# Mixture-of-experts products in units of 32 tokens over four column groups, tokens 33 to 64 under a branch

## The chip, the cores and the metric

The kernel runs on one core of one Trainium2 chip. The metric is the device time of one execution in microseconds (us), lower is better; the figure given for the kernel before is the median of three runs.

## What is computed

One layer of a hybrid network is applied to two groups of 128 tokens (a prompt and a sample), 256 tokens of width 1024 in all, in float32. Modulated norm, one input projection, three token mixers, gates, an output projection; then a second norm and a mixture of experts, a residual and a final norm. The part that the change touches is the mixture:

```python
logits = (t @ router_w + router_b).astype(F32)
top_v, top_i = lax.top_k(logits, TOP_K)            # 4 of 32 experts
probs = jax.nn.softmax(top_v, axis=-1)
...
gu = t @ wgu + bgu                                  # 1024 -> 2048
gate = jnp.minimum(gate, SWIGLU_LIMIT)
up = jnp.clip(up, -SWIGLU_LIMIT, SWIGLU_LIMIT)
act = (up + 1.0) * (gate * jax.nn.sigmoid(SWIGLU_ALPHA * gate))
out = act @ wdn + bdn                               # 1024 -> 1024
acc + wt[:, None].astype(t.dtype) * out
```

256 tokens with 4 experts each are 1024 places, 32 to an expert on average. The weights of one expert are 8 MiB (gate and up) and 4 MiB (down). The router of the reference, on the inputs that the reference draws by default, gives these token counts, in the order in which the kernel takes the experts (i = 0 to 31): 8, 45, 23, 21, 4, 32, 45, 46, 16, 25, 20, 70, 33, 34, 15, 10, 58, 73, 46, 28, 20, 9, 21, 15, 104, 14, 48, 28, 34, 40, 16, 23. Of i = 1 to 31, 18 experts have at most 32 tokens, 10 have 33 to 64 and 3 have more than 64 (i = 11, 17, 24).

## The kernel before

The first 340 us of the span compute everything up to the router. Then the experts follow one another (loop over `EXPERTS`, L1632 on). Their weights come in slabs of 1 MiB ([128, 2048] float32), 8 `gu` and 4 `dn` slabs an expert, all issued from SP in this order. The slabs go through a ring (`Ring`, L169): the slots of SBUF given to it by `start` and the `ring.give` lines are 0 to 11, 15 and 20 to 22, 16 slots. `ring.done` (L198) hands a slot back, and the next slab's DMA is issued on SP into it; that DMA waits for the last product that read the slot. So SP runs 16 slabs, one and a third experts, ahead of the slots that TensorE gives back.

TensorE (PE) takes the weights as the moving operand and the tokens as the stationary one. `gather` builds the expert's tokens, transposed, from `Pq`, a one-hot of the token's rank among the expert's tokens, for 64 ranks (`one_hots`, L1405). `gate_up` (L1491) with n = 64 uses the array as two column groups of 64: each of the four 512-column quarters of a slab is one product of 64 tokens, two of them side by side. With n = 32 it uses four column groups of 32. The products run in two halves of KS = 4 slabs (L1639). After each half `beyond` (L1621) asks for a register value `nu` (L1630, the number of further units of 32 tokens beyond the first 64): with nu = 0 nothing is done, with nu = 1 the stage `more_in` runs for 32 more tokens, with nu of 2 or more for 64 more. Then come `swiglu` (L1465, DVE and ACT), the transposition of the hidden values (`tr` and `copy` into `AT`, L1662), `down2` (L1517, n = 64: 64 columns, the two halves of the contraction in the two column groups), `beyond` with `more_out`, and `halves` (L1615), which scales the sums into a high and a low part; `scatter` (L1472) adds them to the tokens' sums in PSUM banks 4 to 7 one expert later. The first expert (i = 0, NR = 1) has a form of its own, `first_in`, without branches in it; all its tokens beyond 64 are done at the end (`all_once_more`, L1572, at i = 31).

Each branch stands on all engines. On PE, DVE and ACT the path that skips a body is a jump that first waits for the engine's own work before it (`UNCONDITIONAL_BRANCH [waits PE_49]` below).

## Time and profile before

| | us |
|---|---|
| median of 3 runs | 1371.79 (1369.27 to 1374.49) |
| the profiled execution | 1371.8 |
| its span (first to last instruction) | 1370.0 |
| PE busy in the span | 1247.5 (91%) |
| DVE, ACT busy | 418.2 (31%), 241.6 (18%) |
| HBM read | 472.61 MB, 346 GB/s over the span |
| mean granted TensorE clock | 0.981 of full speed |

In the trace PE is matrix products and PEld the loading of their stationary operand; SPq is SP's queue, which issues the DMAs. A float32 product of 512 columns shows as two records, so `gate_up` with n = 64 leaves 8 records a slab, and so does n = 32. L273 is the helper that records every product, L262 every transposition, L256 every DMA; which product it is has to be read from the tiles and shapes (`128*64 128x512` is 64 tokens against 512 columns).

### The profile page before, as it was taken

The numbers are of one execution on the slowest core, as the hardware profiler recorded it, in microseconds if no ns is written. First come the engines' busy times: TensorE is split into PE (matmuls) and PEld (weight loads), VectorE is DVE, ScalarE is ACT, GpSimd is POOL, SyncE is SP. The second block draws the span as 40 slices with busy tenths as digits, with TensorE's granted clock in tenths as the row PEclk, the third lists the DMA queues.
The fourth block names the chain that finished last, engine by engine and source line by source line (L and its number), as shares of the span: only waits on it lengthen the run. The fifth ranks groups of instructions, "written<-read, shape, count | busy, mean of one in ns | idle before, by whom it ended". The sixth has DMA issues, their size and how long they took to land. (4 is left out here: it accounts for less than half of the span.)

```text
span 1370.0 us, 18609 instructions
## 1 busy us (share of the span) xinstructions
PE 1247.5 (91%) x7146; PEld 645.4 (47%) x7146; DVE 418.2 (31%) x858; ACT 241.6 (18%) x490; POOL 42.1 (3%) x69
## 2 busy tenths in 40 slices
PE   5999789999999999999999999999999989999994
PEld 3677678898433344433334434243433343433331
DVE  7768769655111121111121112021211120211113
ACT  4463132233211111111111111011111100111111
POOL 1000101201000000000000000000000000000001
PEclk9999989999999999999999999999999999999997
DMA  9956796865899999999999999989999995999991
GB/s 278 339 180 216 115 318 232 259 242 219 333 384 417 367 415 417 415 415 415 416 401 370 415 416 417 415 346 402 417 415 414 414 395 193 412 414 415 415 407 41
DMA packets 124829, 477.02 MB, mean 348 GB/s; under 512 B 11871, under 2 KB 49505, under 8 KB 90864
## 3 DMA queue, kind: packets, MB, share of 16 engines
q1 hardware_dynamic: 121744, 468.25, 87.9%
q0 software_dynamic: 2288, 5.76, 1.4%
q8 instruction: 118, 1.93, 0.6%
q10 hardware_dynamic: 624, 0.63, 0.1%
q14 instruction: 55, 0.45, 0.1%
HBM read 472.61 MB, written 1.61 MB: 346 GB/s over the span
## 5 line engine op out<-in xcount | busy, mean ns | idle before, releaser
L273 PE MATMUL pb<-sl,sl 128*64 128x512 f32 (+5 forms) x5024 | 959.2, 507 | 32.1 <-PEq L1623 14.5
L273 PEld LDWEIGHTS pb<-sl,sl 128*64 128x64 f32 (+2 forms) x5024 | 431.9, 147 | 515.8 <-issue 450.5
L304 ACT ACTIVATE sl<-sl 128x512 f32<-128x512 f32 (+5 forms) x131 | 72.6, 564 | 559.2 <-DVE sl L279 496.0
L279 DVE TENSOR_SCALAR sl<-pb 128x512 f32<-128x512 f32 (+1 forms) x35 | 23.6, 676 | 434.5 <-PE pb L273 434.5
L287 DVE SCALAR_TENSOR_TENSOR sl<-pb,wsl,sl 128x512 fp32r<-128x512 f32 x64 | 47.6, 750 | 311.1 <-ACT sl L304 309.8
L304 ACT ACTIVATE sl<-pb 128x512 f32<-128x512 f32 (+6 forms) x125 | 68.6, 586 | 215.4 <-PE pb L273 194.0
L262 PE MATMUL pb<-cst,sl 128*128 128x128 f32 (+2 forms) x354 | 53.8, 282 | 28.1 <-DMA sl<-ssm_b_re 8.4
L304 ACT ACTIVATE sl<-pb,wsl 128x512 fp32r<-128x512 f32 x64 | 43.6, 688 | 201.7 <-PE pb L273 198.8
L273 PE MATMUL pb<-hb,sl 128*128 128x128 f32 x512 | 69.7, 291 | 8.4 <-DVE hb L291 8.0
L273 PE MATMUL pb<-sl,PT 128*128 128x512 f32 x256 | 76.3, 420 | 0.5 <-PEq L1623 0.5
L291 DVE TENSOR_TENSOR sl<-sl,sl 128x512 fp32r<-128x512 f32 (+3 forms) x80 | 65.1, 833 | 32.9 <-ACT sl L304 30.9
L273 PEld LDWEIGHTS pb<-hb,sl 128*128 128x128 f32 x512 | 65.8, 203 | 18.9 <-ACT wsl L304 12.7
L262 PEld LDWEIGHTS pb<-cst,sl 128*128 128x128 f32 (+2 forms) x354 | 40.5, 149 | 47.0 <-issue 14.3
L287 DVE SCALAR_TENSOR_TENSOR hb<-sl,taps,hb 128x256 f32<-128x256 f32 x120 | 49.8, 477 | 0.3
L273 PEld LDWEIGHTS pb<-sl,PT 128*128 128x128 f32 x256 | 45.1, 196 | 7.8 <-ACT sl L304 1.3
L291 DVE TENSOR_TENSOR sl<-PWT,sl 128x1024 f32<-128x1024 f32 x32 | 37.8, 1219 | 6.8 <-PE pb L273 6.7
L273 PEld LDWEIGHTS pb<-comb,hb 128*128 128x128 f32 x128 | 19.2, 202 | 43.9 <-DVE sl L279 41.3
L273 PE MATMUL pb<-comb,hb 128*128 128x1 f32 x128 | 21.6, 237 | 17.7 <-PEq L1623 15.9
L273 PE MATMUL pb<-ha,selb 128*64 128x512 bf16 (+1 forms) x140 | 21.4, 390 | 17.1 <-PEq L1623 14.0
L291 POOL TENSOR_TENSOR sl<-sl,sl 128x512 f32<-128x512 f32 (+3 forms) x11 | 16.4, 1503 | 671.3 <-DVE sl L291 656.4
L291 DVE TENSOR_TENSOR sl<-sl 128x512 f32<-128x512 f32 (+4 forms) x79 | 35.3, 464 | 4.5 <-ACT wsl L304 0.5
L273 PE MATMUL pb<-sl,cs 128*32 128x256 f32 (+1 forms) x320 | 30.4, 439 | 0.7 <-PEq L1623 0.7
(170 smaller groups left out, 403.9 us busy)
## 6 DMA issues: line engine op xcount, KB each, us to landing
sl<-w_gate_up SPq DMA_DIRECT2D x256, 1024.0 KB, 13.9
sl<-w_down SPq DMA_DIRECT2D x128, 1024.0 KB, 16.5
sl<-w_mod SPq DMA_DIRECT2D x24, 1024.0 KB, 9.6
sl<-w_in SPq DMA_DIRECT2D x20, 1024.0 KB, 10.8
sl<-w_out SPq DMA_DIRECT2D x4, 1024.0 KB, 12.9
sl<-md POOLq DMA_DIRECT2D x6, 512.0 KB, 9.0
sl<-w_four SPq DMA_DIRECT2D x2, 1024.0 KB
sl<-Kd SPq DMA_DIRECT2D x16, 128.0 KB, 9.0
```

Source lines behind the costliest of these rows:

```text
L262: return sch.op("P", 0.107 * in_.shape[0] / 128, [out], [in_], lambda: te.transpose(out, in_, ident[:in_.shape[0], :in_.shape[0]]))
L273: lambda: te.matmul(out, lhsT, rhs, start=start, stop=stop, skip_group_check=True))
L279: return sch.op(e, c, [o], ap, lambda: ENG[e].tensor_scalar(o, a, s1, None, op0=op0))
L287: lambda: ENG[e].scalar_tensor_tensor(o, a, sc, b, op0=op0, op1=op1))
L291: return sch.op(e, c, [o], [a, b], lambda: ENG[e].tensor_tensor(o, a, b, op=op))
L304: [a] + [x for x in (bias, scale) if hasattr(x, "tensor")], lambda: s.activation(o, a, func, **kw))
```

## The change

For i = 1 to 31 an expert's gate and up products run with n = 32, in one PSUM bank, and tokens 33 to 64 run as a second unit of 32 under a branch of their own (`nu > 0`), with their bias, their own half of the SwiGLU (`glu32(1)`) and of the transposition (`hidden(1)`). `nu` now counts the units beyond the first 32, so that the stages beyond 64 tokens stand under nu > 1 and nu > 2 and do what they did. The down products have two forms: `down2` with 64 columns where there are tokens 33 to 64, `down32` otherwise, which puts the sums of four parts of the contraction into four groups of 32 rows. For that `Pq` gets a second row of ones for experts of at most 32 tokens (`second_row`, four DVE operations per pair of experts, from `rank2` and `far`). The register of the next expert is loaded right after the SwiGLU of the present one (`later = units(...)`). The code of the first expert stays.

```diff
         tt(rank[:, :, :], PB[2][:, 0:64].rearrange("p (g e) -> p g e", g=2), self_[:, :, :], OP.add)
+        far = sm.tile([128, 32], F32, name="far", tag="zi")
+        ts(far[:, :], PB[2][:, 64:96], 32.0, 1000.0, op0=OP.is_gt, op1=OP.mult)
...
+        def second_row(b):
+
+            for a, e in enumerate(EXPERTS[2 * b:2 * b + 2]):
+                if 2 * b + a >= NR:
+                    for g in range(2):
+                        stt(Pq[:, b % 2, a, g], cst[:, C_IOTA:C_IOTA + 128], rank2[:, g, e:e + 1], Pq[:, b % 2, a, g],
+                            op0=OP.is_equal, op1=OP.add)
...
-            ts(nuf[:, :], cntf[:, :], 64.0, None, op0=OP.is_gt)
-            for u in range(1, 6):
-                stt(nuf[:, :], cntf[:, :], 64.0 + 32 * u, nuf[:, :], op0=OP.is_gt, op1=OP.add)
+            ts(nuf[:, :], cntf[:, :], 32.0, None, op0=OP.is_gt)
+            for u in range(1, 7):
+                stt(nuf[:, :], cntf[:, :], 32.0 + 32 * u, nuf[:, :], op0=OP.is_gt, op1=OP.add)
             vcopy(nui[:, :], nuf[:, :])
...
+            stt(rank2[:, :, :], rank[:, :, :], 32.0, far[:, None, :].to_broadcast([128, 2, 32]), op0=OP.add, op1=OP.add)
+            second_row(0)
...
         def beyond(nu, stage):
 
-            with tc.If(nu > 0, preferred_fallthrough_block=False):
-                with tc.If(nu > 1) as more:
+            with tc.If(nu > 1, preferred_fallthrough_block=False):
+                with tc.If(nu > 2) as more:
                     stage(64)
                 with more.Else():
                     stage(32)
 
         def units(e):
-            return nc.values_load(nui[0:1, e:e + 1], min_val=0, max_val=6)
+            return nc.values_load(nui[0:1, e:e + 1], min_val=0, max_val=7)
+
+        def glu32(u):
+
+            c = slice(256 * u, 256 * u + 256)
+            swiglu(GA[:, c], UP[:, c], SG[:, c], PB[u][:, 0:256], PB[u][:, 256:512])
+
+        def hidden(u):
+
+            for h in range(2):
+                tr(PB[2][:, u * 256 + h * 128:u * 256 + h * 128 + 128], GA[:, u * 256 + h * 128:u * 256 + h * 128 + 128])
+            copy(AT.rearrange("p (j c t) -> p j c t", j=2, c=4)[:, :, :, 32 * u:32 * u + 32],
+                 PB[2][:, u * 256:u * 256 + 256].rearrange("p (c j t) -> p j c t", c=4, j=2))
+
+        def down32(sl, j, bk):
+            for w in range(2):
+                for half in range(2):
+                    q, h = 2 * half + j // 2, j % 2
+                    c = half * 1024 + w * 512
+                    mm(bk[w][32 * q:32 * q + 32, :], AT[:, j * 128 + half * 64:j * 128 + half * 64 + 32], sl[:, c:c + 512], h == 0, h == 1)
 
         for i, e in enumerate(EXPERTS):
             b, a = i // 2, i % 2
@@ -1635,16 +1667,27 @@
             if i < NR:
                 first_in(e, x)
             else:
-                bias_in(e, 64, PB)
+                nu = later
+                bias_in(e, 32, PB)
                 for k in range(0, 8, KS):
-                    for q in range(k, k + KS):
-                        gate_up(ring.get(("gu", e, q)), 64, x[:, q], q, PB)
-                    if k == 0:
-                        nu = units(e)
-                    beyond(nu, lambda n: more_in(e, n, range(k, k + KS)))
-                    for q in range(k, k + KS):
+                    ks = range(k, k + KS)
+                    for q in ks:
+                        gate_up(ring.get(("gu", e, q)), 32, x[:, q, 0:32], q, PB)
+                    with tc.If(nu > 0, preferred_fallthrough_block=False):
+                        if k == 0:
+                            bias_in(e, 32, PB[1:])
+                        for q in ks:
+                            gate_up(ring.get(("gu", e, q)), 32, x[:, q, 32:64], q, PB[1:])
+                        if k + KS == 8:
+                            glu32(1)
+                    beyond(nu, lambda n: more_in(e, n, ks))
+                    for q in ks:
                         ring.done(("gu", e, q))
-            swiglu(GA, UP, SG, PB[0][:, :], PB[1][:, :])
+                glu32(0)
+            if i < NR:
+                swiglu(GA, UP, SG, PB[0][:, :], PB[1][:, :])
+            if i < 31:
+                later = units(EXPERTS[i + 1])
             for g in range(2):
                 mm(PB[2][:, 0:1], Pq[:, b % 2, a, g], comb[:, g, e:e + 1], g == 0, g == 1)
                 tr(PB[3][:, g * 128:(g + 1) * 128], Pq[:, b % 2, a, g])
@@ -1659,9 +1702,12 @@
             if i == 31:
                 scatter(i - 1, 1)
                 all_once_more()
-            for j in range(4):
-                tr(PB[2][:, j * 128:(j + 1) * 128], GA[:, j * 128:(j + 1) * 128])
-            copy(AT, PB[2][:, :])
+            if i < NR:
+                for j in range(4):
+                    tr(PB[2][:, j * 128:(j + 1) * 128], GA[:, j * 128:(j + 1) * 128])
+                copy(AT, PB[2][:, :])
+            else:
+                hidden(0)
             if 0 < i < 31:
                 scatter(i - 1, 1)
             if i == 3:
@@ -1671,14 +1717,22 @@
                 for g in range(2):
                     for n in range(2):
                         mm(Y[2 * g + n], combT[:, g * 128:(g + 1) * 128], bdn[:, n * 512:(n + 1) * 512], False)
+            if i < NR:
+                for j in range(4):
+                    down2(ring.get(("dn", e, j)), 64, AT, j, PB[2:4])
+            else:
+                with tc.If(nu > 0, preferred_fallthrough_block=False) as big:
+                    hidden(1)
+                    for j in range(4):
+                        down2(ring.get(("dn", e, j)), 64, AT, j, PB[2:4])
+                with big.Else():
+                    for j in range(4):
+                        down32(ring.get(("dn", e, j)), j, PB[2:4])
+                beyond(nu, lambda n: more_out(e, n))
             for j in range(4):
-                down2(ring.get(("dn", e, j)), 64, AT, j, PB[2:4])
-                if i < NR:
-                    ring.done(("dn", e, j))
-            if i >= NR:
-                beyond(nu, lambda n: more_out(e, n))
-                for j in range(4):
-                    ring.done(("dn", e, j))
+                ring.done(("dn", e, j))
+            if a == 1 and b + 1 < 16:
+                second_row(b + 1)
             halves(a)
             if i == GI:
                 bg, rg = ga2[:, 0:256], ga2[:, 256:512]
```

The first place is PE at the first half of an expert's gate and up products: pb_93 to pb_96 are PSUM banks 0 to 3, the other names slots of weights (sl_76, ...) and token tiles. Before, from the first slab to the branch:

```order
L273 MATMUL pb_93<-sl_76,sl_2673 64x512 [waits DMAHW7_49]
L273 MATMUL pb_93<-sl_76,sl_2673 64x512
L273 MATMUL pb_94<-sl_76,sl_2673 64x512 x2
L1630 TENSOR_LOAD nui
L1623 COMPARE_AND_BRANCH
L1623 UNCONDITIONAL_BRANCH [waits PE_49]
```

In the changed kernel, the same half, with one slab of the first unit, the second unit's branch and the branch for more than 64 tokens:

```order
L273 MATMUL pb_93<-sl_73,sl_2675 32x512 [waits DMAHW3_49]
L273 MATMUL pb_93<-sl_73,sl_2675 32x512 x3
L1676 COMPARE_AND_BRANCH
L1676 UNCONDITIONAL_BRANCH [waits PE_49]
L273 MATMUL pb_94<-ha,selb 32x512 [waits DVE_49]
L273 MATMUL pb_94<-sl_73,sl_2675 32x512 x4
L1676 UNCONDITIONAL_BRANCH
L1636 COMPARE_AND_BRANCH
L1636 UNCONDITIONAL_BRANCH [waits PE_49]
```

Four products of 64 columns a slab became four of 32, in one bank and side by side; the same four stand again in a body that is entered for more than 32 tokens; and there are two branches where there was one. The register is no longer loaded here.

The second place is PE at the down products of an expert. In the changed kernel, from the branch on, the first slab of either form:

```order
L1724 COMPARE_AND_BRANCH
L273 MATMUL pb_95<-sl_76,sl_2686 32x512 [waits DMAHW7_49,Activation_49]
L273 MATMUL pb_95<-sl_76,sl_2686 32x512
L273 MATMUL pb_96<-sl_76,sl_2686 32x512 x2
L1724 UNCONDITIONAL_BRANCH
L262 MATMUL pb_95<-cst,sl_2686 128x128 [waits Activation_49]
L273 MATMUL pb_95<-sl_76,sl_2686 64x512 [waits DMAHW7_49,Activation_49]
L273 MATMUL pb_96<-sl_76,sl_2686 64x512 x2
```

The form for at most 32 tokens is fallen into, the form of before stands behind it with the second transposition ahead of it, and the waits for the slabs' DMAs stand in both.

## Rows read from the trace of the kernel before

**Rows 1.** Busy time by stretch of the span; last columns granted clock, DMA share, GB/s.

```profile
core 0: us, PE busy (x) PEld busy (x) DVE busy (x) ACT busy (x) POOL busy (x), PEclk, DMA share, GB/s
340.00:386.00 46.00, 42.24 (x208) 18.51 (x210) 8.59 (x27) 7.87 (x15) 0.55 (x1) 0.96 0.81 310
...
456.00:470.00 14.00, 13.55 (x54) 3.92 (x54) 1.50 (x2) 1.37 (x2) 0.00 (x0) 0.82 0.78 294
470.00:716.00 246.00, 229.08 (x1180) 94.91 (x1176) 41.27 (x70) 29.58 (x59) 0.00 (x0) 1.00 1.01 414
716.00:760.00 44.00, 40.79 (x247) 17.96 (x248) 5.36 (x9) 3.54 (x7) 2.57 (x5) 1.00 0.94 380
...
896.00:940.00 44.00, 42.46 (x210) 18.19 (x211) 6.33 (x12) 5.00 (x10) 0.00 (x0) 0.98 0.89 357
...
1120.00:1164.00 44.00, 40.18 (x178) 17.44 (x178) 9.22 (x18) 4.55 (x9) 0.00 (x0) 0.92 0.59 227
1164.00:1326.00 162.00, 150.64 (x756) 61.88 (x754) 26.86 (x40) 20.63 (x41) 0.00 (x0) 1.00 1.02 415
...
1338.40:1353.00 14.60, 10.88 (x37) 3.27 (x36) 0.17 (x1) 1.38 (x3) 0.00 (x0) 0.77 0.01 3
1353.00:1370.00 17.00, 2.50 (x8) 1.34 (x8) 11.88 (x23) 4.60 (x11) 5.88 (x4) 0.67 0.17 62
```

**Rows 2.** Timeline of PE, an expert of 32 tokens (i = 5): start, length, group.

```profile
495.19 0.62 PE L273 MATMUL pb<-ha,selb 128*64 128x512 bf16 x4 [0.44 <-PEq L1623]
...
495.65 7.03 PE L273 MATMUL pb<-sl,sl 128*64 128x512 f32 x32
...
503.21 7.09 PE L273 MATMUL pb<-sl,sl 128*64 128x512 f32 x32 [0.53 <-PEq L1623]
...
510.74 0.38 PE L273 MATMUL pb<-comb,hb 128*128 128x1 f32 x2 [0.44 <-PEq L1623]
...
515.60 7.09 PE L273 MATMUL pb<-sl,sl 128*64 128x512 f32 x32
...
523.12 0.62 PE L273 MATMUL pb<-ha,selb 128*64 128x512 bf16 x4 [0.44 <-PEq L1623]
```

**Rows 3.** Timeline of PE, the expert of 73 tokens (i = 17) to the next.

```profile
864.68 0.62 PE L273 MATMUL pb<-ha,selb 128*64 128x512 bf16 x4 [0.56 <-PEq L1623]
865.13 7.03 PE L273 MATMUL pb<-sl,sl 128*64 128x512 f32 x32
872.10 1.92 PE L273 MATMUL pb<-sl,Pg 128*32 128x512 f32 x8
...
875.95 14.21 PE L273 MATMUL pb<-sl,sl 128*32 128x512 f32 x96
...
907.02 5.38 PE L273 MATMUL pb<-sl,sl 128*32 128x512 f32 x32
912.33 3.71 PE L273 MATMUL pb<-sl,PwT 128*128 128x512 f32 x8
915.97 0.62 PE L273 MATMUL pb<-ha,selb 128*64 128x512 bf16 x4
```

**Rows 4.** Timeline of PE, the expert of 104 tokens (i = 24): its start, the next expert's.

```profile
1087.50 0.62 PE L273 MATMUL pb<-ha,selb 128*64 128x512 bf16 x4 [0.43 <-PEq L1623]
...
1149.91 0.62 PE L273 MATMUL pb<-ha,selb 128*64 128x512 bf16 x4
```

**Rows 5.** Waits: who waited for whom, us in total, times, longest.

```profile
SPq L256 <- PEq L1623: 446.9, 76, 18.1
...
PEld pb L273 <- DMA sl<-w_gate_up: 20.3, 38, 1.5
```

**Rows 6.** Timeline of PE at the end: the last expert and the last scatter.

```profile
1328.16 7.09 PE L273 MATMUL pb<-sl,sl 128*64 128x512 f32 x32 [0.65 <-PEq L1623]
...
1341.49 0.81 PE L262 MATMUL pb<-cst,sl 128*128 128x128 f32 x4 [2.88 <-DVEq L1575]
1342.99 9.86 PE L273 MATMUL pb<-sl,sl 128*64 128x512 f32 x32 [0.69 <-ACTq L1623]
1353.31 2.55 PE L273 MATMUL pb<-sl,PT 128*128 128x512 f32 x8 [0.45 <-PEq L1623]
```

**Rows 7.** Groups of instructions by shape: busy, mean ns of one, idle before.

```profile
L291 DVE TENSOR_TENSOR sl<-sl,w 128x128 f32<-128x128 f32 x32 | 9.2, 288 | 0.5
```

More of the change, by code (lines that the diff above doesn't have):

```diff
@@ L576, in build @@
         A8i = sm.tile([128, 2, 8, 4, 2], F32, name="A8i")
-        zi = sm.tile([128, 32], I32, name="zi")
+        zi = sm.tile([128, 32], I32, name="zi", tag="zi")
         def vexp(o, x, n, r, p):
@@ L1281, in build @@
         lg = sm.tile([128, 2, 32], F32, name="lg")
-        cadd = sm.tile([128, 64], F32, name="cadd")
+        cadd = sm.tile([128, 64], F32, name="cadd", tag="cadd")
         c2 = sm.tile([2, 64], F32, name="c2", tag="rank")[:, :]
@@ L1422, in build @@
         comb = sm.tile([128, 2, 32], F32, name="comb")
+        rank2 = sm.tile([128, 2, 32], F32, name="rank2", tag="cadd")
         nui = sm.tile([1, 32], I32, name="nui")
@@ L1547, in further_in @@
             act2(32)
-            v.tensor_copy(at2[:, bass.ds(u * 256, 256)], PB[2][:, 0:256])
+            v.tensor_copy(at2[:, bass.ds(u * 256 - 256, 256)], PB[2][:, 0:256])
         def further_out(e, slab, u):
@@ L1552, in further_out @@
             ts(rr[:, :], rr[:, :], -32.0, None, op0=OP.add)
-            v.tensor_copy(AT[:, 0:256], at2[:, bass.ds(u * 256, 256)])
+            v.tensor_copy(AT[:, 0:256], at2[:, bass.ds(u * 256 - 256, 256)])
             for j in range(4):
@@ L1561, in once_more @@
             slabs = expert_slabs(e)
-            with tc.If(nu > u0):
+            with tc.If(nu > u0 + 1):
                 for part, some in (further_in, slabs[:8]), (further_out, slabs[8:]):
@@ L1568, in once_more @@
                     first_row(e, u0)
-                    with tc.For_i(u0, nu, 1) as u:
+                    with tc.For_i(u0 + 1, nu, 1) as u:
                         part(e, again.get, u)
@@ L1574, in all_once_more @@
             slots = list(ring.free)
-            with tc.If(nc.values_load(numax[0:1, 0:1], min_val=0, max_val=8) > 2):
+            with tc.If(nc.values_load(numax[0:1, 0:1], min_val=0, max_val=9) > 3):
                 keep = o2, at2
```

## Prediction

> **What bounds the kernel now.** I read the busy shares by stretch first. Behind the first 386 us almost nothing but experts is left, and in the long stretches of it the transfers stand at a share of 1.01 to 1.02 and 414 to 415 GB/s, while TensorE is busy some 93% of the time [rows 1]. So two things are close to a limit at once, and the question is which of them the time hangs on where. The timeline of TensorE answers for one expert: from the bias of one ordinary expert to that of the next are 523.12 - 495.19 = 27.9 us [rows 2]. Its weights are 12 slabs of 1.049 MB; at 0.414 MB per us that is 30.4 us, 2.53 a slab. Ordinary experts thus go faster on TensorE than their weights arrive. An expert with more than 64 tokens doesn't: 915.97 - 864.68 = 51.3 us for 73 tokens [rows 3], 1149.91 - 1087.50 = 62.4 for 104 [rows 4]. Then slots are not given back, SP waits for TensorE (446.9 us in all, against 20.3 in which TensorE's loads waited for gate and up slabs [rows 5]), and the transfers pause.
>
> The pauses are seen in the same table. A stretch at less than 415 GB/s has lost its length times (1 - rate/415): 4.1 us at 456 to 470 (i = 3, where the products with the down biases stand in the way), 3.7 at 716 to 760, 6.1 at 896 to 940 and 19.9 at 1120 to 1164, behind the experts of 70, 73 and 104 tokens; and 11.6 before 386 [rows 1]. Over the rest TensorE could be twice as fast and nothing would be gained, since the transfers run without a pause. At the end the transfers stop at 1338.4, and TensorE still works on the last expert until 1352.9 [rows 1, 6].
>
> **The change on TensorE.** Eight slabs with 32 tokens and four with 64 took 14.21 us together [rows 3]; four with 64 take 7.09 [rows 2], so four slabs in the new form cost 3.56. An expert of at most 32 tokens saves 2 x 3.5 there. Its down form was seen too: 5.38 instead of 7.09 [rows 3], less than half saved, since one slab's products go to two of the four groups. SwiGLU and transposition on half the columns save TensorE about 1 us of waiting, the narrower bias at most the half of 0.62 [rows 2]. Against it stand three more skipped or taken branches: a skipped one costs 0.44 to 0.53 now [rows 2], a second in a row finds the engine empty already, so I take 1 us for the three; an entered one showed no gap (872.10 follows the end of 865.13 + 7.03 [rows 3]). The register load that moved behind the SwiGLU stands on all engines, where before it hid under products; one place shows such a load with its branches in the open, 2.88 us at the last expert [rows 6]. Bounds are 0 and 2.9; I take 0.5, because behind one load no stack of jumps follows here. Together 27.9 - 7.0 - 1.7 - 1.2 + 1.0 + 0.5 gives about 19.5 to 21 us for each of the 18 small experts; I use 21.
>
> An expert of 33 to 64 tokens runs two units, 2 x 3.56 per half, as long as before; it adds a second bias (0.6), the branches (1), the load (0.5) and a second transposition and copy in front of its down products (about 1): 31 us. The three large ones get the same 3 us: 54 and 65.
>
> The four operations of `second_row` are of the size of one that takes 288 ns [rows 7], 1.2 us on DVE per pair. They stand ahead of `halves` but behind nothing late: the down products of 5 us cover them. If that cover goes, 0.6 us an expert appear. The operations at the router (`far` ahead of the first one-hots, `rank2`, two of `second_row`) put perhaps 0.3 us on the path to the first expert.
>
> **What that is worth.** On TensorE the sum falls, 31 experts from 28 x 27.9 + 2 x 51.3 + 62.4 = 946 us to 18 x 21 + 10 x 31 + 2 x 54 + 65 = 861; the transfers need 31 x 30.4 = 942 either way. So from the second expert on the transfers set the pace, TensorE waits for each slab, and the gain is only what the transfers lost, plus the end.
>
> - Pause at i = 3: two small experts, 21 us each, come before; gone, -4.1.
> - The large ones. If an expert starts when its first slab has landed, at T, the other 15 slots are already asked for: transfers until T + 38. An expert of 73 tokens gives back its first four slots at about T + 21 (four slabs at 2.53, second unit, gathering as in rows 3, extra unit), the next four by T + 33, the last by T + 54; each four are 10 us of transfers, so they run to T + 68 without a pause. The next expert starts at T + 58 and frees slots from T + 67 on; if it has 33 to 64 tokens, as it has twice, it is as slow as its weights and a pause of 1 to 3 us comes later. I leave 1.5 of 3.7 and 3.5 of 6.1: -2.2 and -2.6.
> - With 104 tokens the last slots come back from T + 61 on, 3 us late, plus 2 us until a transfer is under way, and the following expert's first about 3 late: I leave 8 of 19.9, -11.9.
> - The end. The last gate-and-up slab lands four slabs, 10.2 us, before the last down slab. After it come one slab's products (0.9), the branches and the middle part, 1342.99 - 1328.16 - 7.09 = 7.7 now, 1.3 less with half the columns [rows 6]: ready about 2 us before the last slab. The down form takes 5.38, or 5.38 x 9.86/7.09 = 7.5 if the clock is as low there as now (0.77 in that stretch [rows 1]). The products end 3.5 to 5.5 us after the last transfer instead of 14.5: -9. The rest of the end, 17 us to 1370, stays.
> - The second expert has 45 tokens and gives its slots back about 1 us later, and the router's 0.3: +1.2, at a place where the transfers pause.
>
> Sum: -4.1 - 2.2 - 2.6 - 11.9 - 9 + 1.2 = -28.6. The profiled execution took 1371.8, which is the median of the runs (1371.79); 1371.8 - 28.6 = **1343**. The low end is every large expert's pause gone (another 13) and 3 more at the end: 1326.
>
> **Rivals.**
> *TensorE starves and loses its clock* (0.17). What the rows show: the clock is at half, 1.2 instead of 2.4 GHz, in parts of stretches in which the products are thin or wait (granted 0.82 at 456 to 470, 0.77 behind 1338.4), and 1.00 where TensorE is busy throughout [rows 1]. After the change 0.9 us of products are followed by 1.6 us of waiting for the next slab. One such fall cost 9.86 - 7.09 = 2.8 us [rows 6]. One in every expert makes the small ones 24 us, still under 30.4, but those of 33 to 64 tokens 34 and the large ones 57 and 68. Rows of two to four experts that are slower than their weights (45, 46; 70, 33, 34; 58, 73, 46) then hand a lag of 3.6 us each on to the large ones: some 4 us more of pause at each of the three, 4 at the end: 1343 + 16, about 1360. Against it: a late TensorE is a busy one, and busy stretches have full clock. The Trainium skill, page "TensorE: Matmul & The Clock Gate", section "HAM oscillation — how this bites in real kernels", says that short bursts of products between waits for transfers fall back to the lower clock in each wait and start cold again. By that rule this is the case that comes; the two low stretches agree with it in kind, but neither follows a wait for a slab.
>
> *The branches cost more than the products save: slower* (0.06). The place is the three more branch points and the exposed register load in each expert, on PE, DVE and ACT alike; behind them stand the next unit's products and the SwiGLU. If each costs what the dearest row shows (2.88 [rows 6]) and not 0.3 to 0.5, an expert has some 9 us more: 18 x 30 + 10 x 40 + 2 x 63 + 74 = 1140 against 946 now, over 1500 us. It decides from about 2.7 us more per expert than I count: 861 + 31 x 2.7 = 945 is today's sum. At 4 us more the sum is 985, 39 over today's, less 9 at the end: about 1400. Against it: the skipped branches cost 0.44 to 0.65 [rows 2, 3, 6].
>
> *The pauses aren't TensorE's* (0.09). If SP's own order (each DMA stands behind the branches on SP) made them, only the end is gained: 1371.8 - 9 + 1.2 = 1364, or 1366 to 1369 with a low clock there. Rows 5 speak against it.
>
> *The tokens aren't so distributed* (0.02). With most experts over 32 tokens nothing falls on TensorE, and it is as now.
>
> **How the numbers follow.** Forecast 0.66, the rivals as given. Half a per cent, 6.9 us, is about what a measurement of this kernel can tell from no change. Faster by more than that: the forecast, nearly all of the first rival and half of the third, 0.84; within it 0.08; slower 0.08, the second rival and a clock that falls harder. The range 1326 to 1364 holds the forecast with its low end, most of the first rival and half of the third.
>
> **What would show it.** Right: the dips at 456, 716 and 896 gone or under 3.5 us, about 8 left behind the expert of 104; many waits of TensorE for slabs of w_gate_up and w_down, where there are few now; small experts 30.4 us apart with 16 to 21 us of products; last landing near 1318, the last down products within 6 us behind it. Wrong: TensorE still without waits for slabs, gaps of over 1 us behind the new branches, or granted clock below 0.8 over whole experts with the dips still there.

## The result and the profile after

The changed kernel takes **1402.68 us** (median of 4 runs, 1397.2 to 1415.93) against 1370.53 of the kernel before beside it: ratio **1.0233, 95% interval 1.0203 to 1.0263**. It is slower by 32 us where 28.6 less were forecast, outside the range of 1326 to 1364.

First the page of the kernel before and then that of the changed one: busy time, and the row of the queue that fetches TensorE's instructions (packets, MB, share).

```profile
PE 1247.5 (91%) x7146; PEld 645.4 (47%) x7146; DVE 418.2 (31%) x858; ACT 241.6 (18%) x490; POOL 42.1 (3%) x69
...
q8 instruction: 118, 1.93, 0.6%
```

```profile
span 1399.4 us, 21272 instructions
...
PE 1148.1 (82%) x7994; PEld 605.3 (43%) x7994; DVE 422.2 (30%) x975; ACT 238.4 (17%) x516; POOL 42.1 (3%) x69
...
q8 instruction: 144, 2.36, 0.7%
```

TensorE's busy time did fall, by 1247.5 - 1148.1 = 99.4 us. Its idle time rose by more: 1399.4 - 1148.1 = 251.3 against 1370.0 - 1247.5 = 122.5, so +128.8. The difference is the 29.4 us by which the span grew. Now the same stretches as [rows 1], columns as there.

```profile
456.00:470.00 14.00, 8.84 (x75) 3.32 (x76) 3.14 (x8) 0.46 (x2) 0.00 (x0) 0.93 1.03 413
470.00:716.00 246.00, 196.16 (x1325) 80.84 (x1327) 39.32 (x92) 28.17 (x64) 0.00 (x0) 0.91 1.01 411
716.00:760.00 44.00, 38.85 (x326) 17.18 (x322) 5.88 (x13) 3.86 (x9) 2.57 (x5) 0.92 0.84 338
760.00:896.00 136.00, 104.38 (x676) 44.63 (x672) 19.90 (x47) 13.94 (x32) 0.00 (x0) 0.85 0.97 392
896.00:940.00 44.00, 39.79 (x265) 16.30 (x258) 9.36 (x25) 5.29 (x12) 0.00 (x0) 0.96 0.71 280
940.00:1120.00 180.00, 140.29 (x945) 60.09 (x943) 26.87 (x62) 19.50 (x45) 0.00 (x0) 0.89 0.96 392
1120.00:1164.00 44.00, 39.03 (x220) 16.81 (x222) 9.12 (x20) 3.68 (x9) 0.00 (x0) 0.96 0.90 367
1164.00:1326.00 162.00, 132.92 (x910) 54.41 (x910) 26.80 (x61) 19.55 (x44) 0.00 (x0) 0.96 0.95 384
```

The dip at 456 is gone, as forecast. The dips behind the experts of 70 and 73 tokens have grown; the one behind the expert of 104 tokens, which ends later here, is about half as large (34 us from 1150 to 1184 at 287 GB/s, 10.5 us lost, 19.9 before). Stretches that lost next to nothing before now lose too (760 to 896 and 940 to 1120, at 416 and 413 GB/s before, and behind 1184): by length times (1 - rate/415) these rows from 470 to 1326 lose 2.4 + 8.2 + 7.5 + 14.3 + 10.0 + 5.1 + 12.1 = 60 us of transfers, where the three dips of before lost 29.7. The clock is below full in every stretch. The wait rows say who is waited for (us, times, longest).

```profile
PE pb L273 <- issue: 76.5, 20, 7.0
...
PEld pb L273 <- DVEq L1636: 40.0, 13, 4.0
...
PE pb L273 <- PEq L1636: 31.6, 39, 3.0
...
PE pb L273 <- DVEq L1636: 28.5, 14, 3.1
...
PEld pb L273 <- DMA sl<-w_gate_up: 21.3, 22, 2.3
...
SPq L256 <- PEq L1636: 353.5, 61, 15.8
```

The waits for gate and up slabs, which were to become many, stand at 21.3 us as before [rows 5]. At the top is a row that the kernel before lacks: 20 times, 76.5 us in all, TensorE idles though nothing in the profile holds it. L1636 is the helper of the branches. Where these gaps lie shows in TensorE's timeline, i = 14 (15 tokens) and the start of i = 15.

```profile
785.94 0.40 PE L273 MATMUL pb<-ha,selb 128*32 128x512 bf16 x4 [0.57 <-PEq L1636]
786.17 3.61 PE L273 MATMUL pb<-sl,sl 128*32 128x512 f32 x32
792.37 1.90 PE L273 MATMUL pb<-sl,sl 128*32 128x512 f32 x2 [2.59 <-PEq L1636]
797.56 6.14 PE L273 MATMUL pb<-sl,sl 128*32 128x512 f32 x30 [3.30 <-issue]
810.53 0.56 PE L273 MATMUL pb<-comb,hb 128*128 128x1 f32 x2 [6.83 <-issue]
...
817.84 5.38 PE L273 MATMUL pb<-sl,sl 128*32 128x512 f32 x32
823.79 0.40 PE L273 MATMUL pb<-ha,selb 128*32 128x512 bf16 x4 [0.57 <-PEq L1636]
```

Four slabs take 3.61 us and the down products 5.38, as priced. But this expert lasts 823.79 - 785.94 = 37.9 us, not 21. At the two places where the bodies for tokens 33 to 64 and beyond 64 are skipped stand gaps of 2.59 and 6.83 us; the one of 3.30 us stands two records behind the first of them, among the products of the next half, where nothing is skipped. The gap of 6.83 us in the view of the transfers (803.5 to 810.6; queue, packets, MB, share):

```profile
q1 hardware_dynamic: 407, 2.94, 99.7%
q8 instruction: 1, 0.02, 0.9%
```

One packet of 16 KB of instructions is fetched in it. I counted TensorE's gaps over 0.9 us between 386 and 1370, and those with such a packet in flight: before 5 gaps of 10.2 us in all, one of them (2.9) with a fetch; after 61 gaps of 157.7, 30 of them (107.6 us) with a fetch. This counts a gap whatever ends it, but in 29 of the 30 the next product comes 1.2 to 2.4 us after the packet has landed. Eight of the 30 are of 6.3 to 7.0 us, 52.2 us together, with the packet starting inside the gap; the others are 1.4 to 4.5 us, with a packet that was under way when the gap began or started soon after.

### The profile page after: what moved, and what is told of

It is laid out like the page before. It is cut to its first block, busy times and chain, and to the rows that moved or that the text cites. A ratio compares the mean times of both kernels' runs of the same rounds, so it can differ in the third digit from the quotient of the medians.

```text
span 1399.4 us, 21272 instructions
## 1 busy us (share of the span) xinstructions
PE 1148.1 (82%) x7994; PEld 605.3 (43%) x7994; DVE 422.2 (30%) x975; ACT 238.4 (17%) x516; POOL 42.1 (3%) x69
## 5 line engine op out<-in xcount | busy, mean ns | idle before, releaser
L273 PE MATMUL pb<-sl,sl 128*32 128x512 f32 (+5 forms) x5856 | 836.7, 536 | 106.6 <-issue 62.4
L273 PEld LDWEIGHTS pb<-sl,sl 128*32 128x32 f32 (+2 forms) x5856 | 365.8, 132 | 520.9 <-issue 458.0
L304 ACT ACTIVATE sl<-sl 128x256 f32<-128x256 f32 (+5 forms) x144 | 71.4, 504 | 564.4 <-DVE sl L279 501.6
L279 DVE TENSOR_SCALAR sl<-pb 128x256 f32<-128x256 f32 (+1 forms) x48 | 20.9, 435 | 428.2 <-PE pb L273 424.1
L304 ACT ACTIVATE sl<-pb 128x512 f32<-128x512 f32 (+4 forms) x138 | 66.9, 518 | 247.6 <-PE pb L273 217.8
L273 PE MATMUL pb<-hb,sl 128*128 128x128 f32 x512 | 88.1, 342 | 7.5 <-DVE hb L291 6.5
L273 PEld LDWEIGHTS pb<-hb,sl 128*128 128x128 f32 x512 | 86.7, 257 | 17.0 <-ACT wsl L304 9.6
L273 PE MATMUL pb<-ha,selb 128*32 128x512 bf16 (+1 forms) x192 | 19.7, 386 | 19.2 <-PEq L1636 11.4
L287 DVE SCALAR_TENSOR_TENSOR hb<-cst,rank,hb 128x128 f32<-128x128 f32 x62 | 17.7, 347 | 55.0 <-PE pb L273 54.9
L291 DVE TENSOR_TENSOR sl<-sl 128x256 f32<-128x256 f32 (+4 forms) x92 | 32.5, 369 | 5.8 <-ACT sl L304 0.5
```

The source lines that it names most:

```text
L273: lambda: te.matmul(out, lhsT, rhs, start=start, stop=stop, skip_group_check=True))
L279: return sch.op(e, c, [o], ap, lambda: ENG[e].tensor_scalar(o, a, s1, None, op0=op0))
L287: lambda: ENG[e].scalar_tensor_tensor(o, a, sc, b, op0=op0, op1=op1))
L291: return sch.op(e, c, [o], [a, b], lambda: ENG[e].tensor_tensor(o, a, b, op=op))
L304: [a] + [x for x in (bias, scale) if hasattr(x, "tensor")], lambda: s.activation(o, a, func, **kw))
```

## Experiments

Gaps are counted as above, up to 1370 us (in e4, e6, e9 and e11 to the end of the products). "Idle" is span less PE busy.

### One form beyond 64, and nothing beyond 64

e1 drops the inner choice of `beyond`; e2 and e3 leave the stage out, in the changed kernel (`return` at its head) and in the kernel before.

```diff
             with tc.If(nu > 1, preferred_fallthrough_block=False):
-                with tc.If(nu > 2) as more:
-                    stage(64)
-                with more.Else():
-                    stage(32)
+                stage(64)
```

> The changed kernel, but with the stage for more than 64 tokens in its 64-token form alone, so that half of the code that most experts skip is gone (the experts of 70 and 73 tokens do 32 columns more than they need, about 9 us each). Theory 1, the code: TensorE's own instructions, fetched in blocks of 16 KB through the same DMA engines as the weights, arrive too late where an expert runs little of the code it passes; then the 108 us of gaps with a fetch in them fall under 40 us, the blocks from 144 to about 108, and the time to 1345 to 1365. Theory 2, the clock: TensorE waits for slabs, falls to half clock and stays late; the waits are the same, so at least 1390. Theory 3, the second unit of 32 and its branches cost more than counted: the same 33 to 64 experts, about 1400.

> The changed kernel without the stages for more than 64 tokens: the tokens from the 65th on are left out of their expert's products (three experts). Theory 1, the code: about 70 blocks instead of 144, gaps with a fetch in them under 15 us, transfers without a pause from the second expert on, 1315 to 1340. Theory 2, the clock: only the work of three experts goes, waits for slabs and half clock stay, 1370 to 1390. Theory 3, the second unit: 1370 to 1390.

> The kernel before without the stages for more than 64 tokens (left out of the products of three experts): the partner of the run above. All theories: the three pauses of the transfers go, TensorE at 27 to 28 us an expert stays just under the transfers' 30.4, 1325 to 1340; no clock falls in the middle. Theory 1: its difference to the run above is small, within 15 us. Theories 2 and 3: the run above is slower by 40 us or more.

e1: **1372.8** us, ratio 1.0022 (1.0005 to 1.0038), 112 blocks of instructions instead of 144, gaps with a fetch 23 and 45.0 us, none over 2.7 us. Theory 1 comes nearest, but both numbers lie a little above what it allowed. With *more* work for the large experts (51 to 53 us for i = 11 and 17, where the changed kernel takes 45, from the one-column products of the expert before to its own) 30 us come back. e2: **1328.95**, ratio 0.9696 (0.9675 to 0.9717), 81 blocks, 17.5 us in such gaps. e3: **1320.95**, ratio 0.9648 (0.963 to 0.9666), a little under its range of 1325 to 1340. So without the large experts the change is no gain either, it is 8 us worse. The rows of e2, waits and then the long stretch of [rows 1]:

```profile
PE pb L273 <- DMA sl<-w_gate_up: 126.2, 112, 3.7
```

```profile
470.00:716.00 246.00, 201.76 (x1326) 76.45 (x1320) 38.39 (x88) 27.78 (x64) 0.00 (x0) 0.88 1.02 416
```

This is the state that the forecast described, TensorE waiting for slabs at 416 GB/s. Its granted clock there is 0.88, lower than the changed kernel's 0.91, and it costs at most the 8 us by which e2 is behind e3, since the transfers set the pace.

### Code that is never entered, added to the kernel before

If the passed code costs, it must cost in the old form too. Behind each half of the gate-and-up products of the kernel before stands a branch for more tokens than any expert has, its body once (e6), three times (e4) and nine times (e9) four slabs: 64, 192 and 576 TensorE instructions at 62 places.

```diff
+                    with tc.If(nu > 5, preferred_fallthrough_block=False):
+                        for _ in range(3):
+                            for q in range(k, k + KS):
+                                gate_up(ring.get(("gu", e, q)), 64, x[:, q], q, PB)
```

> The kernel before with one more branch per half of an expert's gate and up products, over a body of 48 products that is never entered (192 instructions, about 12 KB): only code that is passed is added, no work, no other clock. Theory 1, the code: about 160 blocks, gaps with a fetch in them appear where there is one now, 1385 to 1430. Theories 2 and 3: 62 skipped branches of 0.2 us, at most 1385, and no gap with a fetch.

> The kernel before with the same two never-entered branches per expert as in the run that took 1634.9, but with a third of the body (64 instructions, the size of one half of the second unit). Theory 1, the code: about 134 blocks and far less than a third of the loss, 1380 to 1450, with some 20 to 80 us of gaps that hold a fetch. Theory 3, the branches themselves: their number is the same, so again about 1600.

> The kernel before with the never-entered branch of the earlier run behind each gate/up half, its body nine times four slabs in the 64 form, 576 TensorE instructions (2.25 blocks of 16 KB), where that run had 192. Theory J (a taken branch whose target lies in a block that is not there costs one wait of some 6.3 us, however much is passed): one gap per branch at most, none over 7 us, 62 x up to 6.3 us, so 1700 to 1780 us; block count up by clearly less than 140. Theory S (every block passed is fetched in turn and pays): 62 x 576 / 256 = 140 more blocks than the kernel before (258 in all), gaps with two or three fetches in them of 8 to 20 us, at some 5.0 us a block 2000 us or more.

Measured: e6 **1478.8** us, ratio 1.0785 (1.0751 to 1.0818); e4 **1634.88**, 1.1931 (1.1908 to 1.1955); e9 **1877.82**, 1.3716 (1.367 to 1.3762). e4 lies far above the range of either theory, e6 some 30 us above. All four kernels execute the same 7146 products:

| | idle us | PE busy us | clock | blocks | gaps with a fetch |
|---|---|---|---|---|---|
| before | 122.5 | 1247.5 | 0.981 | 118 | 1, 2.9 us |
| e6, 64 | 197.4 | 1280.5 | 0.955 | 134 | 18, 49.4 us |
| e4, 192 | 309.2 | 1324.3 | 0.913 | 165 | 40, 190.6 us |
| e9, 576 | 492.8 | 1381.7 | 0.857 | 245 | 69, 407.3 us |

e6's row for the new branch, beside that of the branch that it follows (waits):

```profile
PE pb L273 <- PEq L1645: 59.9, 54, 1.2
...
PE pb L273 <- PEq L1623: 15.2, 28, 0.7
```

A second skipped branch in a row makes the gap 59.9/54 = 1.11 us, one alone 15.2/28 = 0.54: +0.57. From e6 to e4 no branch is added, only 31 blocks of code, and the time rises by 156 us, 5.0 a block. 62 x 192/256 = 46.5 blocks of code were added in e4, and 47 more are fetched; in e9 it is 127 of 140 added. A body of e9 is 2.25 blocks long, so at least one block of each holds nothing but skipped code: such blocks are mostly fetched too. But the wait is one per jump. TensorE's timeline of e4 and of e9, and the packets in the e9 gap:

```profile
582.49 2.83 PE L273 MATMUL pb<-sl,sl 128*64 128x512 f32 x6 [6.39 <-issue]
```

```profile
623.59 2.83 PE L273 MATMUL pb<-sl,sl 128*64 128x512 f32 x6 [7.71 <-issue]
```

```profile
q8 instruction: 2, 0.03, 3.1%
```

With the transfers at a share of 1.0 most such gaps are 6.0 to 6.6 us with one block (21 in e4, one of them 5.5 and one 7.05), and 7.7 to 8.2 with two, which travel together. e4 also has nine gaps of 3.9 to 4.2 us with one block, in which the transfers stood at a share of 0.4 to 0.7. One of either kind, as stretches:

```profile
453.60:460.10 6.50, 0.00 (x0) 0.00 (x0) 0.00 (x0) 0.00 (x0) 0.00 (x0) 0.77 1.01 421
469.10:473.20 4.10, 0.00 (x0) 0.00 (x0) 2.67 (x4) 0.63 (x1) 0.00 (x0) 1.00 0.56 191
```

 So e9 fell between the theories, with a single gap (13.7 us) that held three fetches; and its time was over J's because of the clock. The table gives that part: the same products take 33, 77 and 134 us longer, 0.36 to 0.44 us for each us of added idle time.

### Is it the branches themselves

e5 moves `beyond` inside the body for tokens 33 to 64, at all three places, so an expert of at most 32 tokens passes one branch where it passed two.

```diff
-                    beyond(nu, lambda n: more_in(e, n, ks))
+                        beyond(nu, lambda n: more_in(e, n, ks))
...
-                beyond(nu, lambda n: more_out(e, n))
+                    beyond(nu, lambda n: more_out(e, n))
```

> The changed kernel with the branch for more than 64 tokens inside the body for more than 32, at all three places, so that an expert of at most 32 tokens jumps once where it jumped twice, over the same code. Theory 1, the code that is passed: blocks as before the edit (about 144), the gaps with a fetch stay at 80 us or more, 1385 to 1402. Theory 3, the number of branches: 18 small experts lose three jumps with their waits each, 1360 to 1380 and the gaps under 50 us.

**1398.83** us, ratio 1.0175 (1.0109 to 1.0241), 144 blocks, gaps with a fetch 31 and 108.7 us. Fewer branches over the same code: nothing measurable in the time. TensorE's idle time at skipped branches (its row <- PEq L1636) does fall, from 31.6 to 11.8 us, but its waits for gate and up slabs rise from 2.9 to 20.2, and the gaps with a fetch stay. The number of branches alone doesn't make the loss; what they jump over stays with it.

### Less to transfer

Does the fetch wait because it queues behind the slabs? And what bounds the two kernels? From the fourth expert on each slab's load brings half of its bytes (e8 the kernel before, e7 the changed one).

```diff
-            r = [(("gu", e, k), lambda sl: sl[:, :], A["w_gate_up"][0, e, k * 128:(k + 1) * 128, :]) for k in range(8)]
+            n = 2048 if e in EXPERTS[:3] else 1024
+            r = [(("gu", e, k), lambda sl: sl[:, 0:n], A["w_gate_up"][0, e, k * 128:(k + 1) * 128, 0:n]) for k in range(8)]
...
```

> The kernel before with half of the bytes of each slab left out from the fourth expert on (the other half of a slot holds what an earlier expert left there, so the outputs are not the reference's); every instruction of the engines stands as it was. Baseline for the next run. The transfers then need some 15 us per expert and TensorE's 27.9 us set the pace: the pauses of the kernel before (4.1, 3.7, 6.1, 19.9 us) and part of the end go, so some 1330 to 1355 us. Both theories expect that; if it stays at 1371, the transfers did not bound anything.

> The changed kernel with the same half of each slab's bytes left out. Theory A (code passed late because its 16 KB blocks queue behind saturated slab transfers): with the queues half empty a block lands soon, the gaps with a fetch in them (30 of them, 107.6 us, in the changed kernel) shrink to under 40 us in all, and the kernel is 50 to 90 us faster than the same cut of the kernel before, 1260 to 1300 us. Theory B (passing code costs its time whatever the transfers do): the gaps stay near 100 us and it is within 30 us of the same cut of the kernel before, 1330 us or more. Theory C (half clock from idle time): as B in time, but with gaps under 60 us and the loss in stretches at half clock.

e8: **1370.85** us, ratio 1.0 (0.9983 to 1.0017). Half the bytes, and nothing changes, against what both theories expected. The long stretch again:

```profile
470.00:716.00 246.00, 229.54 (x1178) 96.08 (x1176) 41.27 (x70) 29.59 (x59) 0.00 (x0) 0.99 0.65 212
```

At 212 GB/s instead of 414 TensorE is as busy as in [rows 1]. **The kernel before hangs on TensorE alone**, with the transfers just able to follow. e7: **1365.69**, ratio 0.9975 (0.9948 to 1.0002), gaps with a fetch 29 and 96.0 us, the full ones still 6.0 to 6.6. That looked like theory B; but inside such a gap the transfers were no fewer (stretches of e7: the long one, and the gap at i = 9, of 25 tokens):

```profile
470.00:716.00 246.00, 202.62 (x1438) 80.35 (x1436) 39.53 (x92) 27.73 (x62) 0.00 (x0) 0.94 0.63 211
```

```profile
595.90:602.40 6.50, 0.01 (x2) 0.01 (x3) 0.00 (x0) 0.00 (x0) 0.00 (x0) 0.75 1.01 323
```

A share of 0.63 on average, 1.01 just there: the slabs come in bursts. So the same cut again with n = 256, an eighth: e10 the changed kernel, e11 the kernel before with e4's code, e12 the kernel before.

> The changed kernel with only an eighth of each slab's bytes loaded from the fourth expert on (256 columns of a gate/up slab, the like of a down slab; the rest of a slot holds an earlier expert's). With half of the bytes the full gaps were still 6.0 to 6.6 us, but the transfers stood at a share of 0.89 to 1.01 inside those very gaps, so theory A (the block queues behind slab transfers) wasn't excluded. With an eighth a slab's bursts are short. Theory A: full gaps shrink to under 4 us and those with a fetch to under 50 us in all; time 1290 to 1330 us. Theory B (a fixed wait for a jump to a block that is not loaded): gaps of 6 us and some 90 us in all stay, 1350 to 1370 us.

> The kernel before with the never-entered bodies of 192 instructions, and the same eighth of each slab's bytes. With full slabs it took 1634.88 us, with 40 gaps of 190.6 us that have a fetch in them, the full ones 6.1 to 6.5 us. Theory A: full gaps under 4 us, 1480 to 1560 us. Theory B: the same gaps, 1610 to 1640 us.

> The kernel before with the same eighth of each slab's bytes from the fourth expert on: the baseline of the two runs before (1322.62 us for the changed kernel so cut). If TensorE alone sets the time of the kernel before, as the half cut said, it stays at 1360 to 1372 us, and the change, with its waits for code shortened by free queues, is 40 to 50 us faster than it. If transfers still held the kernel before back, it falls to 1320 to 1340 and the change is level with it or slower.

e12: **1371.23**, ratio 1.0 (0.9982 to 1.0019). e11: **1558.34**, 1.1369 (1.1327 to 1.141), 77 us below e4; gaps with a fetch 35 and 124.7 us for 40 and 190.6. e10: **1322.62**, 0.9644 (0.9615 to 0.9672); gaps with a fetch 17 and 48.5 us. The place at i = 9 again, timeline and stretch:

```profile
582.41 3.61 PE L273 MATMUL pb<-sl,sl 128*32 128x512 f32 x32
590.10 2.79 PE L273 MATMUL pb<-sl,sl 128*32 128x512 f32 x12 [4.08 <-issue]
```

```profile
586.00:590.00 4.00, 0.02 (x4) 0.00 (x0) 0.00 (x0) 0.00 (x0) 0.00 (x0) 0.88 0.20 45
```

With the queues at a share of 0.2 the full gaps are 3.6 to 4.4 us, in e10 as in e11, where they were 6.0 to 7.0. Both theories were half right: some 3.8 us of a jump are a fixed wait, some 2.5 a place in the queue behind slabs. For the change this decides the sign. With free queues it gains 1371.23 - 1322.62 = **48.6 us**; with the full ones it loses 32. Of the 76.5 us between the spans of the changed kernel and of e10, 61.9 are gaps with a fetch (110.4 to the end of the span, less 48.5) and 1148.1 - 1126.7 = 21.4 busy time (granted clock 0.926 and 0.939); the rest, -7, are other gaps.

### What can be saved

i1 takes e1 and e5 together, makes the SwiGLU of tokens 33 to 64 unconditional and moves the register load behind the first scatter; i2 keeps both forms beyond 64; i3 is i1 with all eight slabs in one stage; i4 is i1 with a product of zeros per slab to keep TensorE busy.

```diff
-                        if k + KS == 8:
-                            glu32(1)
...
                 glu32(0)
+                glu32(1)
```

> Put together: the 64-token form alone beyond 64 tokens, nested branches, the second half of the SwiGLU for every expert and outside the branch (for at most 32 tokens its result is not used), and the register of the next expert loaded behind the first scatter. Theory 1 and the 1.9 us waits of TensorE for DVE's branch behind the SwiGLU: gaps with a fetch under 40 us, experts of 33 to 64 tokens 1.5 to 3 us shorter, 1340 to 1362, faster than the kernel before. If neither counts: 1372 as without nesting.

> The same with both forms beyond 64 tokens, as in the change. Theory 1: the code is back, about 143 blocks, so 20 to 35 us over the run with one form, 1370 to 1395. If the waits behind the SwiGLU and the register were what the change lost: 1345 to 1365, as with one form.

> The run with one form for tokens beyond 64, nested, and the first SwiGLU of tokens 33 to 64 in its own branch, now with all eight gate/up slabs in one stage instead of two of four: half of the gate/up branches go, the code stays as long. If the skipped branches by themselves cost (0.6 to 1.2 us each on TensorE, 62 fewer), 1340 to 1358 us. If the code's blocks cost, 1360 to 1370, as its parent's 1365. If holding eight slabs until the end of the stage starves the ring, slower, 1370 to 1385.

> The same parent (1365) with one product of zeros more per gate/up slab of each small expert (512 columns into a bank that the 33-to-64 branch sets anew), to keep TensorE busy where it would wait. It adds some 2 to 7 us of TensorE per expert, which fits below 30.4 us only where no gap stands. If half clock in the lagging stretch costs (theory C), the clock rises from 0.93 and the time falls below 1358. If the blocks of code cost, the added products come on top: 1368 to 1400.

i1: **1365.41**, ratio **0.9959 (0.9938 to 0.9981)**, 112 blocks, 21 gaps with a fetch and 42.1 us. It beats both kernels, the kernel before by 0.4%. Here the count says too much: 13 of the 21 end when a slab lands, and a packet only happens to be in flight. TensorE's waits for gate and up slabs are 76.6 us in i1, against 2.9 in the changed kernel and 2.4 in the kernel before:

```profile
PE pb L273 <- DMA sl<-w_gate_up: 76.6, 70, 3.2
```

 i2: **1382.87**, 1.0099 (1.0055 to 1.0142), 144 blocks, 36 and 109.1 us. Against i1 the second form beyond 64 costs 17 us, though it makes the large experts faster. Against the changed kernel i2 is 20 us faster with the same blocks and as much in gaps with a fetch. So nesting, the unconditional SwiGLU and the later register load are worth 20 us together; e5, the nesting alone, gained nothing measurable. In an expert of 33 to 64 tokens TensorE's wait behind the SwiGLU is 0.66 us in i2, 1.93 in the changed kernel. i3: **1407.78**, 1.0276 (1.0238 to 1.0314), the "slower" case and more; fewer gaps with a fetch (15), but mostly whole ones (63.8 us), and slots come back four slabs later; how the 42 us divide was not tried. i4: **1426.07**, 1.0401 (1.0361 to 1.0441), above its range. Its clock is back at 0.978 and up to 1370 us *no* gap has a fetch in it (behind that, in the last expert, two of 6.2 us together), but PE busy is 1295.2 against i1's 1164.2. The same code can be fetched without a visible wait when TensorE has more work between the jumps; these products cost more than they hid.

## Why the prediction was wrong

**The step that failed is the price of the branches**, "three more skipped or taken branches ... I take 1 us for the three". It priced the jump and not the code behind it. With the 0.5 for the register load it allowed 1.5 us an expert, some 46 us over 31; TensorE's idle time grew by 128.8, hardly any of it for slabs. Four things stand in its place. A second skipped branch adds 0.57 us, where a third of 1 us was taken (e6). A jump whose target block is not there yet costs some 3.8 us, and 6.0 to 7.0 while slabs fill the queues (e4, e7, e10, e11); with the shorter gaps behind such jumps these are 107.6 us over 30 gaps, where before had 2.9. The waits of the branches on other engines, with the register load, are part of the 20 us between the changed kernel and i2. And slow products follow: behind each of the eight gaps of over 6 us the clock stands at half. Its own sign of being wrong, "gaps of over 1 us behind the new branches", is what the trace shows. Stretches and timeline of the changed kernel at its last expert:

```profile
1350.00:1356.00 6.00, 3.16 (x25) 0.87 (x24) 0.00 (x0) 0.00 (x0) 0.00 (x0) 1.00 1.01 408
...
1360.00:1364.00 4.00, 4.00 (x20) 0.95 (x24) 0.00 (x0) 0.00 (x0) 0.00 (x0) 0.50 0.75 300
```

```profile
1359.96 6.54 PE L273 MATMUL pb<-sl,sl 128*32 128x512 f32 x32 [6.31 <-issue]
```

Granted 1.00 ahead of the gap of 6.31 us, 0.50 behind it, and 6.54 us for four slabs that take 3.61 at full clock. Over the whole span TensorE is busy for 147.6 us in stretches at half clock, before for 29.6; half of the difference, 59 us, is what the clock cost: an estimate. By e4's and e6's 0.41 to 0.44 us per us of idle, the 128.8 us of added idle time would come to 53 to 57. That these gaps make it slower is shown from three sides: code alone makes the kernel before slower (e4), less code makes the changed one faster by 30 us although its products get dearer (e1), and shorter fetches turn its loss into a gain (e10).

The rule that spoke against this change was there to be read, and I missed it. The Trainium skill, page "Runtime: NRT & Kernel Launch", section "Instruction fetch mechanics", says that instructions stream in in blocks of 16 KiB, that crossing a block boundary is mostly hidden, and that a taken branch to a target outside the loaded window has to wait for that block to be fetched. The trace agrees with both halves: 118 blocks with one visible gap before, up to 7.0 us per jump after. The price, and that it hangs on the slab traffic, are the runs' own.

**What bounds the kernel**: for the kernel before the forecast named both, TensorE behind the large experts and the transfers "over the rest", 946 against 942 us in sum; e8 and e12 say TensorE alone. The pauses were read rightly as TensorE holding slots. For the changed kernel it put TensorE at 861, so that "the transfers set the pace". But from the one-column products of i = 1 to those of i = 31 TensorE took 1367.70 - 390.56 = 977 us, where it took 1335.91 - 389.10 = 947 before. In the changed kernel a slab hardly mattered as a thing to wait for; it mattered as traffic that an instruction block stands behind, a part that no step of the forecast gave it. The state that the forecast described does exist, without the large experts (e2: 126.2 us of waits for slabs, 416 GB/s) and, between the large experts, in i1.

**The products** were priced rightly: 3.61 for 3.56, 5.38 for 5.38. **33 to 64 tokens**: 557.57 - 525.84 = 31.7 us for the 31 forecast (middle to middle, i = 6 to 7). That it comes so near is in part luck: its largest piece, 1.93 us of waiting for DVE's queue at L1636 behind the SwiGLU, is not among the forecast's terms. **Large ones**: 51.4 us for 73 tokens and 61.9 for 104, from bias to bias, as before and under the 54 and 65 forecast. **Small experts**: forecast 21; from the one-column products of one to those of the next the shortest took 24.5 (i = 20), 4.5 of it in two gaps with a fetch; i = 14 took 37.9. **Pauses**: the one at i = 3 went as forecast (-4.1). Of the -11.9 behind the expert of 104 tokens 9.4 came (19.9 to 10.5); the -2.2 and -2.6 turned into the opposite, stretches without a pause got some, and in all 30 us more were lost [rows 1 against the table above]: small experts no longer made up what large ones had lost. **The end** (-9): the products were to end 3.5 to 5.5 us after the last transfer. In the changed kernel the transfers run at 300 GB/s until 1364 and at 54 behind it, and the last down products end at 1374.35 + 7.89 = 1382.2, 18 later: the gap of 6.31 us fell into the last expert, and half clock with it.

**The rivals.** *Branches cost more* came true in sign, from another place: I argued against it with rows of skipped branches (0.44 to 0.65), which jump over code too (62 of the 118 blocks are gone in e3), but over code that had come in time, and its price was put at the register load and the branches on all engines. i2 shows that these were part of it, not how much each: the load was not moved alone. That its "about 1400" for 4 us more per expert lies so near to 1402.68 is in part luck, since the fetches are no part of it. *The clock* was right that it falls (0.926, from 0.981), but the cause was different: idle time behind jumps, not waits for slabs. The rule that the forecast cites for it from the Trainium skill, page "TensorE: Matmul & The Clock Gate", section "HAM oscillation — how this bites in real kernels", held in kind. Where the waits were for slabs (e2) a clock of 0.918 cost at most the 8 us between e2 and e3. *The pauses aren't TensorE's*: e8 and e12 exclude it, since the time did not depend on the transfers.

Why i1 stops at 1365 and not nearer e2's 1329 can be read from its transfers. A stretch with a large expert and one without:

```profile
700.00:740.00 40.00, 38.48 (x249) 14.66 (x247) 7.55 (x18) 5.20 (x12) 1.46 (x3) 1.00 0.75 289
740.00:904.00 164.00, 142.86 (x1002) 57.28 (x1001) 31.77 (x73) 18.69 (x44) 1.12 (x2) 0.95 1.01 412
```

They run at 412 to 415 GB/s but for three pauses, this one, 904 to 944 (282 GB/s) and 1132 to 1160 (247), which lose 12.1 + 12.8 + 11.3 = 36 us; e2, without large experts, has none, and i1 takes 36.5 us more. So where most of the code's price is gone, the forecast's state comes, but with larger pauses than its 13 us: a second term that was too small. i1's large experts take 50 to 54 us each in the one form, so that they don't show the changed kernel's own. Still open is how the loss of 32 us divides between fetches and the branches' other waits.

## What to carry to other kernels

Price a branch by the code that it jumps over, on the engine with the most instructions, and dearer where weights fill the transfer queues: count instructions between the branch and its target, and look in the trace for an instruction packet inside a gap without a releaser. A second form for a rare case can cost more at every place that skips it than it saves where it runs; here dropping it gave 17 to 30 us. And halve a suspected bound before building on it: two sums that agree within 0.5% don't tell which one the time hangs on.

## What the hardware showed

- A jump to a block of code that was not loaded left TensorE idle for 3.6 to 4.4 us with the transfer engines at a share of 0.2, for 6.0 to 7.0 at a share near 1, and for 7.7 to 8.2 where two blocks came together (e9). Both lengths stand in one kernel, e4. With free queues the packet mostly starts 1.2 to 1.5 us into the gap, with full ones 3.5 to 4.5; it takes 0.9 to 1.4 us, and the first product comes 1.4 to 1.9 later.
- Blocks that hold only skipped code are mostly fetched as well: 127 of 140 added in e9, where each body of 2.25 blocks has at least one such block.
- The kernel before moves its weights at 414 to 415 GB/s and a share of 1.01 to 1.02 in its long stretches, and yet its time stays the same with seven eighths of them left out from the fourth expert on (e12).
- With more products between the jumps the fetches were all but invisible: 116 blocks in i4, and no gap with a fetch up to 1370 us.
- Behind idle gaps of over 6 us the granted clock was 0.50 in all eight places of the changed kernel, as in the stretch at 1360 above; the products of e4, e6 and e9 took 0.36 to 0.44 us longer per us of added idle time.
